# Merge gates' sigmoids at a fixed place in ScalarE's order, and the first merge gate's load ahead of part of the recurrence's output

## The chip, the cores and the metric

The kernel runs on one core of one Trainium2 chip. The metric is the device time of one execution in microseconds (us), as the median of several runs. A core has five engines that run their own instruction queues in order and meet through semaphores: TensorE (PE in the profile, with PEld for its weight loads), VectorE (DVE), ScalarE (ACT), GpSimd (POOL) and SyncE (SP), which in this kernel issues the DMAs. Matmul results land in eight banks of PSUM.

## The reference

One layer with two token mixers side by side, for 1024 tokens of width 1024, in float32:

```
h = rmsnorm(x, norm_g);  proj = h @ w_in      # split into q, k, v, decay code, gates, logits
o_gla = gla_chunked(...)                      # 4 heads, a recurrence with a decay per channel
o_gla = rmsnorm(o_gla, gla_norm_g) * silu(g_gate);   y_a = o_gla @ w_pa
o_sb = stick_breaking(...)                    # 8 heads, 128-query blocks, strictly causal
o_sb = o_sb * silu(s_gate);                          y_b = o_sb @ w_pb
gates = sigmoid(m_logits + b_gate)            # one gate per branch and channel
merged = gates[0] * y_a + gates[1] * y_b
return rmsnorm(x + merged @ w_o, final_g)
```

What the change touches is the term `gates[0] * y_a`: the sigmoid of the first branch's logits and its product with the projection of the recurrence's output.

## The kernel before

Everything lies transposed, channels on the 128 partitions and tokens along the free dimension, in two halves of 512 tokens. Each float32 operand is split into a rounded high part and a remainder, so that a product is three matmuls (high by high, high by low, low by high); `split` (L163) copies the high part on ACT and takes the difference on DVE.

The program is a chain of stages. An input stage norms and transposes x and projects it; the projections by blocks of two output panels follow (`pair_job`, L233), with the recurrence (`gl_...`, L861 to L1000) woven in. Results wait in DRAM: `d_ga` holds the logits of the first merge gate, `d_ogl` the recurrence's output, `d_q`, `d_k`, `d_v` the operands of the second mixer. Then comes the stage that matters here, the stick-breaking attention (L1025 to L1219), and behind it the two output projections.

The attention runs over 64 steps, 8 heads h by 8 query blocks i (L1205). A step does, in program order:

- every other step, the load of two later blocks' queries (`load_q`, L1021, tile `q`), and at i = 3 the load of the next head's keys and values (`load_head`, L1009 and L1012, tiles `k` and `v`);
- `scores` of the block two steps ahead: matmuls into a bank `z` (L1068 to L1070), in two halves of 320 to 512 columns where the block's prefix is over 512 long, a sigmoid of each half on ACT (L1071, tile `be`), and a running product on DVE (L1074). There are two `z` banks, and a half's bank is free when its sigmoid has run;
- `st.run`, which takes work from a hand-written list, below;
- `turn` of the block i: PE transposes (L1086) into `tr` and `pp` banks, split on ACT and DVE (L164 and L165, tiles `ath`, `atl`, `afh`, `afl`);
- at i = 2 the values of the previous head's second half and at i = 5 those of this head's first half (`values`, L1107 to L1114: matmuls into `av`, a product on DVE, a store to `d_osb`).

The list `line` (L1193 to L1198) is worked off one unit at a time, at i = 3 and i = 6 of heads 0, 1, 2, 4 and 6, and at i = 6 of the others. A unit is one projection of 24 matmuls (L203 to L205, bank `pp`). The entries that are not units (loads) run together with the unit ahead of them. First come four gates of the second mixer (`gate`); then `o_dma(1)`, the load of the second half of the recurrence's output as four transfers of 1 MB (L1189, tiles `oa21h`, `oa21l`, `oa22h`, `oa22l`); then the 16 units `pa(eb, n)`, the projection `y_a` of output panel eb and half n, each of which ends in `ma_half`. The first such unit runs at h = 1, i = 3, and the first that reads `oa21h` and its companions at h = 2, i = 6.

`ma_half` (L1157) first starts the load of the next unit's gate logits (`ga_load`, L1151, DMA at L1155 from `d_ga` into a tile `o`, one of three), then runs the sigmoid in that tile on ACT (L1161), the product with the projection on DVE (L1162), and the store to `d_ma` (L1163). The very first load is an entry of the list.

In this stage the order of the instructions on each engine is settled when the program is built, by a scheduler that works with estimated durations: it may put an instruction ahead of others that stand earlier in the program. The order on each engine is fixed from then on, and an instruction at the head of a queue that has to wait holds up all behind it. The stages behind L1460 are ordered by hand instead.

Of the kernel before, what the change touches and what calls it, by code (L numbers as in the profile page):

```python
# [11 lines left out]
AF = mybir.ActivationFunctionType  # L12
# [90 lines left out]
def hybrid_layer(ctx: ExitStack, tc: tile.TileContext, x, norm_g, w_in, w_up, b_dec,  # L103
# [5 lines left out]
    nc = tc.nc  # L109
# [43 lines left out]
    vcol = const.tile([P, 22], F32, tag="vcol", name="vcol")  # L153
# [13 lines left out]
    def half(n):  # L167
        return slice(n * HALF, (n + 1) * HALF)
# [146 lines left out]
    def quarter(pool, nm, tag):  # L315
        return tuple(pool.tile([P, 4, HALF], F32R, tag=tag + s, name=nm + s, bufs=1) for s in "hl")
# [239 lines left out]
    def silu(v, dst):  # L556
        o = stage().bitcast(F32)
        nc.scalar.activation(o[:, 0], v, AF.Sigmoid)
        nc.vector.tensor_mul(o[:, 1], v, o[:, 0])
        nc.sync.dma_start(dst, o[:, 1])  # L560
# [575 lines left out]
    def load(w, c0, key):  # L1136

        def go():
            raw = wk.pop(0) if wk else None
            ws[key] = load_w(w, c0, raw=raw)  # L1140
            if raw is not None:
                wk.append(raw)

        return (go, False)

    def unit(key, quads, n, fn):
        return (lambda: fn(proj_t(ws[key], quads, n)), True)
# [3 lines left out]
    def ga_load():  # L1151
        if len(ga) < len(halves):
            eb, n = halves[len(ga)]
            ga[eb, n] = stage().bitcast(F32)
            nc.sync.dma_start(ga[eb, n][:, 0], d_ga[eb][:, half(n)])  # L1155

    def ma_half(pt, eb, n):  # L1157

        ga_load()
        o = ga[eb, n]  # L1160
        nc.scalar.activation(o[:, 0], o[:, 0], AF.Sigmoid, bias=vcol[:, eb:eb + 1])  # L1161
        nc.vector.tensor_mul(o[:, 1], pt, o[:, 0])  # L1162
        nc.sync.dma_start(d_ma[eb][:, half(n)], o[:, 1])  # L1163

# [4 lines left out]
    def gate_load(h):  # L1169
        return load(w_in, C_SG + h * P, ("g", h))  # L1170

    def gate(h, n):
        return unit(("g", h), hq, n, lambda pt: silu(pt, d_sg[h][:, half(n)]))

    def pa_load(eb):
        return load(w_pa, eb * P, ("a", eb))

    def pa(eb, n):
        halves.append((eb, n))
        return unit(("a", eb), oq, n, lambda pt: ma_half(pt, eb, n))  # L1180

    def o_dma(n):

        def go():
            for e in range(2):
                nm = f"a{n + 1}{e + 1}"
                oq[n, e] = quarter(a21b if nm == "a21" else hp, "o" + nm, nm)
                for i in range(2):
                    nc.sync.dma_start(oq[n, e][i].bitcast(F32), d_ogl[e][:, i, :, half(n)])  # L1189

        return (go, False)

    line = [gate_load(6), gate_load(7), gate(6, 0), gate(7, 0), o_dma(0), gate(6, 1), pa_load(0), gate(7, 1), o_dma(1),  # L1193
            pa_load(1), (ga_load, False), pa_load(2), pa(0, 0), pa(1, 0), pa(2, 0)]
    for eb in range(5):
        line += ([pa(eb, 0)] if eb > 2 else []) + [pa(eb, 1), pa_load(eb + 3)]
    line += [pa(eb, n) for n in range(2) for eb in range(5, KB)]
# [433 lines left out]
```

## Time and profile before

| | us |
|---|---|
| median of 3 runs | 1179.27 |
| lowest and highest of them | 1178.54 and 1179.57 |
| the profiled execution | 1177.88 |
| its span in the profile | 1176.2 |

The profiled execution's span is the time from its first to its last recorded instruction; 1.7 us lie around it. The granted clock of TensorE over the span is 0.998 of full speed. All times of day below are microseconds from the span's start. In the views, L12 is line 12 of the kernel before; a row of a timeline gives the start, the duration, the engine, the line and operation, output and input tiles, and in brackets how long the engine sat idle before it and what it waited for.

### The profile page before, as it was taken

Reading aid. Unit: us, or ns where it says so; the run is one execution under the profiler, and the core shown is the slowest. Engines: PE = TensorE matmul, PEld = TensorE weight load, DVE = VectorE, ACT = ScalarE, POOL = GpSimd, SP = SyncE. Lnnn points to the kernel's source line nnn. Section 1 sums busy time; section 2 is a strip of 40 time slices with the busy share of each in tenths; the row PEclk is TensorE's granted clock in tenths of the full one; section 3 lists DMA queues with packets and bytes.
Section 4 is the critical chain, followed back from the end, with each engine's and each line's share of the span. In section 5 each row is a group of like instructions: output and inputs, shape, how many; then the busy total and the mean of one; then the engine's idle time right before and its main releaser. Section 6 shows DMA issues by size and latency. Waiting matters only on the chain.

```text
span 1176.2 us, 16650 instructions
## 1 busy us (share of the span) xinstructions
PE 1161.5 (99%) x5823; PEld 978.7 (83%) x5823; DVE 857.9 (73%) x1441; ACT 557.9 (47%) x1046; POOL 243.4 (21%) x217
## 2 busy tenths in 40 slices
PE   8999999999999999999999999999999999999997
PEld 7999888887888888888888878888888888888886
DVE  6797667888676886776665677456777876488986
ACT  6556663433544545545444443344444444364544
POOL 1022232334242242342242232000000000700001
PEclk9999999999999999999999999999999999999999
DMA  7325549997455664654543357789766556848652
GB/s 290 126 63 161 206 164 324 327 312 240 139 179 179 200 212 161 204 177 130 168 138 125 114 174 238 260 309 316 262 200 229 182 175 199 282 160 276 226 197 108
DMA packets 189456, 239.25 MB, mean 203 GB/s; under 512 B 12438, under 2 KB 128300, under 8 KB 187836
## 3 DMA queue, kind: packets, MB, share of 16 engines
q1 hardware_dynamic: 188796, 237.20, 60.8%
q8 instruction: 46, 0.75, 0.3%
q10 hardware_dynamic: 576, 0.98, 0.2%
q14 instruction: 38, 0.31, 0.1%
HBM read 150.06 MB, written 88.08 MB: 202 GB/s over the span
## 4 chain that ended last, share of the span: by engine, by line
PE 95%; DMA 2%; DVE 1%; ACT 1%; issue 1%; SPq 0%; POOLq 0%; POOL 0%; ACTq 0%
PE pp L269 17%; PE pp L270 17%; PE pp L271 17%; PE pp L204 3%; PE pp L203 3%; PE pp L205 3%; PE pp L222 2%; PE tr L1086 1%; PE z L1068 1%; PE av L1109 1%; PE av L1108 1%; PE av L1107 1%; DMA o<-d_ga 1%; PE z L1070 1%; PE z L1069 1%; PE xa L1362 1%
## 5 line engine op out<-in xcount | busy, mean ns | idle before, releaser
L269 PE MATMUL pp<-S,wh 128*128 128x512 f32 x372 | 147.0, 395 | 0.4 <-ACT f L275 0.4
L271 PE MATMUL pp<-S,wl 128*128 128x512 f32 x372 | 145.0, 390 | 0.0
L270 PE MATMUL pp<-S,wh 128*128 128x512 f32 x372 | 144.9, 389 | 0.0
L165 DVE TENSOR_TENSOR wl<-tt,wh 128x1024 fp32r<-128x1024 f32 x62 | 76.6, 1235 | 52.4 <-ACT wh L164 52.1
L308 DVE TENSOR_TENSOR f<-pp,f 128x512 f32<-128x512 f32 x93 | 64.0, 688 | 69.4 <-PE pp L271 63.0
L164 ACT ACTIVATE wh<-tt 128x1024 fp32r<-128x1024 f32 x62 | 65.6, 1059 | 75.0 <-PE pp L270 67.4
L243 POOL TENSOR_TENSOR tt<-raw 128x512 f32<-128x512 f32 x31 | 43.5, 1402 | 260.1 <-DVE wl L165 234.1
L275 ACT ACTIVATE f<-pp 128x512 f32<-128x512 f32 x93 | 55.0, 592 | 79.6 <-PE pp L271 74.1
L1074 DVE TENSOR_TENSOR_SCAN be<-be,m 128x128 f32<-128x128 f32 (+3 forms) x64 | 86.1, 1348 | 4.8 <-ACT be L1071 4.6
L164 ACT ACTIVATE wh<-raw 128x1024 fp32r<-128x1024 f32 (+1 forms) x47 | 48.4, 1030 | 84.6 <-PE pp L270 48.5
L269 PEld LDWEIGHTS pp<-S,wh 128*128 128x128 f32 x372 | 70.5, 189 | 14.7 <-ACT f L275 0.6
L271 PEld LDWEIGHTS pp<-S,wl 128*128 128x128 f32 x372 | 69.8, 188 | 14.8
L270 PEld LDWEIGHTS pp<-S,wh 128*128 128x128 f32 x372 | 69.9, 188 | 13.8
L165 DVE TENSOR_TENSOR wl<-raw,wh 128x1024 fp32r<-128x1024 f32 (+1 forms) x47 | 63.1, 1343 | 18.7 <-ACT wh L164 18.1
L230 POOL TENSOR_TENSOR r<-r,nhalf 128x1 f32<-128x1 f32 x40 | 25.2, 629 | 194.5 <-DVE r L229 194.5
L1268 POOL TENSOR_TENSOR N<-A,A 128x512 f32<-128x512 f32 x4 | 6.7, 1668 | 242.2 <-DMA A<-d_osb 242.2
L1071 ACT ACTIVATE be<-z 128x384 f32<-128x384 f32 (+4 forms) x96 | 46.9, 494 | 20.4 <-PE z L1070 18.3
L269 PE MATMUL pp<-ha11h,wh 128*128 128x512 f32 x124 | 49.2, 397 | 0.0
L269 PE MATMUL pp<-ha12h,wh 128*128 128x512 f32 x124 | 48.9, 395 | 0.0
L269 PE MATMUL pp<-ha22h,wh 128*128 128x512 f32 x124 | 48.7, 393 | 0.0
L164 ACT ACTIVATE dh<-raw 128x512 fp32r<-128x512 f32 x31 | 19.6, 631 | 61.4 <-PE pp L270 61.4
L269 PE MATMUL pp<-S,dh 128*128 128x512 f32 x124 | 48.6, 392 | 0.0
(546 smaller groups left out, 3425.5 us busy)
## 6 DMA issues: line engine op xcount, KB each, us to landing
raw<-in_w_in_dram SPq DMA_DIRECT2D x31, 1024.0 KB, 6.0
d_t<-t SPq DMA_DIRECT2D x16, 512.0 KB, 5.2
d_ogl<-o SPq DMA_DIRECT2D x64, 128.0 KB, 2.4
d_q<-o SPq DMA_DIRECT2D x16, 512.0 KB, 3.2
d_k<-o SPq DMA_DIRECT2D x16, 512.0 KB, 4.7
d_v<-o SPq DMA_DIRECT2D x32, 256.0 KB, 2.3
k<-d_k SPq DMA_DIRECT2D x8, 1024.0 KB, 7.1
v<-d_v SPq DMA_DIRECT2D x16, 512.0 KB, 4.9
```

The costliest lines, as they stand in the source:

```text
L164: nc.scalar.activation(hi, src, AF.Copy)
L165: eng.tensor_sub(lo, src, hi.bitcast(F32))
L203: nc.tensor.matmul(pt, whi[:, kb], h_, start=kb == 0, stop=False)
L204: nc.tensor.matmul(pt, whi[:, kb], l_, start=False, stop=False)
L243: nc.gpsimd.tensor_sub(t1, b[:, 0, 1], b[:, 0, 0])
L269: nc.tensor.matmul(pt, bh[:, j], ah[:, j], start=first and j == 0, stop=False, skip_group_check=True)
L270: nc.tensor.matmul(pt, bh[:, j], al[:, j], start=False, stop=False, skip_group_check=True)
L271: nc.tensor.matmul(pt, bl[:, j], ah[:, j], start=False, stop=j == 3, skip_group_check=True)
L275: nc.scalar.activation(t[nm], t[bank], AF.Copy)
L308: nc.vector.tensor_add(add, bank, add)
L1071: nc.scalar.activation(om[:, off + pc * w:off + (pc + 1) * w], zt[:, 0:w], AF.Sigmoid, scale=-inv_sqrt)
L1074: nc.vector.tensor_tensor_scan(rest, rest, m1[:, off:T][:, ::-1], 1.0, op0=ALU.mult, op1=ALU.max)
```

## The change

Two edits. The first wraps the sigmoid of `ma_half` so that the scheduler keeps it at its place in the program among ACT's instructions, where it stood free before. The second moves two entries of the list: the load of the first gate's logits and the two weight loads that stood behind `o_dma(1)` now stand ahead of it.

```diff
         ga_load()
         o = ga[eb, n]
-        nc.scalar.activation(o[:, 0], o[:, 0], AF.Sigmoid, bias=vcol[:, eb:eb + 1])
+        tc.keep_in_program_order(nc.scalar.activation(o[:, 0], o[:, 0], AF.Sigmoid, bias=vcol[:, eb:eb + 1]))
         nc.vector.tensor_mul(o[:, 1], pt, o[:, 0])
...
-    line = [gate_load(6), gate_load(7), gate(6, 0), gate(7, 0), o_dma(0), gate(6, 1), pa_load(0), gate(7, 1), o_dma(1),
-            pa_load(1), (ga_load, False), pa_load(2), pa(0, 0), pa(1, 0), pa(2, 0)]
+    line = [gate_load(6), gate_load(7), gate(6, 0), gate(7, 0), o_dma(0), gate(6, 1), pa_load(0), gate(7, 1),
+            (ga_load, False), pa_load(1), pa_load(2), o_dma(1), pa(0, 0), pa(1, 0), pa(2, 0)]
```

No instruction is added or removed, and POOL's order stays as it was.

On ACT, the first of the 16 sigmoids, at h = 1, i = 3 (`o<-o,vcol` is the gate's sigmoid, `ath` and `afh` the copies of `turn`, `be` the sigmoids of `scores`; - is the order before, + the order now):

```order
 L1071 ACTIVATE be<-z 128x384
-L164 ACTIVATE ath<-tr 128x4x128
-L1071 ACTIVATE be<-z 128x448
-L1161 ACTIVATE o<-o,vcol 128x512
-L1071 ACTIVATE be<-z 128x448
+L1161 ACTIVATE o<-o,vcol 128x512
+L164 ACTIVATE ath<-tr 128x4x128
+L1071 ACTIVATE be<-z 128x448 x2
```

The gate's sigmoid moved out from between the two halves of a block's scores to a place ahead of the copy of the transposes. Of the other 15, thirteen move to a later place and the last two stay: at i = 3 they now stand between the scores and the copies of `turn`, at i = 6 behind the first scores of the next head and ahead of the copies. The order before had pulled most of them ahead by one to three units, so that the place of the second unit held the third gate's sigmoid and that of the seventh unit, at h = 4, i = 6, the ninth gate's; now each unit holds its own.

On SP's queue, from step 6 of head 0 on (`d_sg` is a store, `v` and the `oa` tiles are loads):

```order
 L1189 DMA oa21h<-d_ogl_137 128x4x512
 L560 DMA d_sg_107<-o 128x512
+L1155 DMA o<-d_ga_139 128x512
 L1189 DMA oa21l<-d_ogl_137 128x4x512
 L1189 DMA oa22h<-d_ogl_138 128x4x512
 L1012 DMA v<-d_v_93 128x1024
 L1189 DMA oa22l<-d_ogl_138 128x4x512
-L1155 DMA o<-d_ga_139 128x512
```

The first gate's load passes three of the four transfers of the recurrence's output and the load of `v` between them; the fourth, `oa21h`, still stands ahead of it. One more pair on SP changes places: a load of keys (`k`, for head 3) now stands behind the store of `d_osb` that followed it.

On PE, one place changes, at i = 1 and i = 2 of head 2 (`av` are the values of the head before, `z` the scores of block 4; the piece ends one row before the old place of the three transposes):

```order
 L1086 MATMUL tr<-ident,be 128x128 x2
+L1068 MATMUL z<-k,q 128x320
+L1069 MATMUL z<-k,q 128x320
+L1070 MATMUL z<-k,q 128x320
 L1107 MATMUL av<-afh,v 128x512
 L1068 MATMUL z<-k,q 128x320
 L1069 MATMUL z<-k,q 128x320
 L1070 MATMUL z<-k,q 128x320
+L1086 MATMUL tr<-ident,be 128x128 x3
 L1108 MATMUL av<-afl,v 128x512
```

Both halves of the scores and the three transposes behind them now come earlier by one matmul of the values. On DVE, the product L1162 changes places with one neighbour at two places: at the first unit it now stands ahead of the remainder of `ath`, and at the twelfth, behind the attention, ahead of a remainder that the next stage reads.

## The prediction

> **What bounds the kernel.** The page first: the busy shares, then the chain of work that ended last.
>
> ```profile
> PE 1161.5 (99%) x5823; PEld 978.7 (83%) x5823; DVE 857.9 (73%) x1441; ACT 557.9 (47%) x1046; POOL 243.4 (21%) x217
> ...
> PE 95%; DMA 2%; DVE 1%; ACT 1%; issue 1%; SPq 0%; POOLq 0%; POOL 0%; ACTq 0%
> ```
>
> PE is the bound nearly everywhere: idle for 1176.2 - 1161.5 = 14.7 us in all. A change on ACT and SP can win only what PE stands still because of them, so the next view is the waits, of ACT over the whole span and then of PE between 770 and 1030 us, the attention and the projections behind it.
>
> ```profile
> ACT o L1161 <- DMA o<-d_ga: 45.1, 14, 6.1
> ...
> PE z L1068 <- ACT be L1071: 1.0, 1, 1.0
> PE tr L1086 <- DVE atl L165: 0.4, 2, 0.2
> ```
>
> The columns are total us, times, longest. ACT waits 45.1 us for the gate's loads, but PE loses only about 1.4 us in these 260. The timeline shows where: PE first, then ACT, then SP.
>
> ```profile
> 817.05 0.48 PE L1068 MATMUL z<-k,q 128*128 128x512 f32 x1
> 817.36 0.39 PE L1069 MATMUL z<-k,q 128*128 128x512 f32 x1
> 817.60 0.40 PE L1070 MATMUL z<-k,q 128*128 128x512 f32 x1
> 818.95 0.50 PE L1068 MATMUL z<-k,q 128*128 128x512 f32 x1 [0.96 <-ACT be L1071]
> 819.29 0.40 PE L1069 MATMUL z<-k,q 128*128 128x512 f32 x1
> ...
> 810.08 0.49 ACT L1071 ACTIVATE be<-z 128x384 f32<-128x384 f32 x1 [3.81 <-PE z L1070]
> 815.56 0.60 ACT L164 ACTIVATE ath<-tr 128x512 fp32r<-128x512 f32 x1 [4.99 <-PE tr L1086]
> 816.17 0.55 ACT L1071 ACTIVATE be<-z 128x448 f32<-128x448 f32 x1
> 817.74 0.72 ACT L1161 ACTIVATE o<-o,vcol 128x512 f32<-128x512 f32 x1 [1.02 <-DMA o<-d_ga]
> 818.37 0.52 ACT L1071 ACTIVATE be<-z 128x448 f32<-128x448 f32 x1
> ...
> 797.88 0.37 SPq L1189 DMA_DIRECT2D oa21h<-d_ogl  x1
> ...
> 801.67 0.43 SPq L1189 DMA_DIRECT2D oa21l<-d_ogl  x1
> ...
> 807.63 0.33 SPq L1012 DMA_DIRECT2D v<-d_v  x1
> 808.01 0.43 SPq L1189 DMA_DIRECT2D oa22l<-d_ogl  x1
> 808.49 0.50 SPq L1155 DMA_DIRECT2D o<-d_ga  x1
> ```
>
> Read backwards: PE's scores of block 7, second half, want the bank that the second half of block 6 holds. That half's sigmoid (818.37) stood behind the gate's sigmoid, which waited for its load. The load was issued at 808.49, behind a `v` load that SP held until 807.63. The chain says the same, with the landing:
>
> ```profile
> 808.49 9.17 DMA o<-d_ga
> ```
>
> So it landed at 808.49 + 9.17 = 817.66.
>
> **The change, part by part.** Part 1, the stop at 818. PE would have started the second half one matmul step behind 817.60, at 817.84 (the step from 817.36 to 817.60 was 0.24), and the next matmul at 818.08; it started at 819.29. The stop, with the restart, costs 819.29 - 818.08 = **1.21 us**. Is anything late in its place? The load now follows the store of `d_sg`, where `oa21l` was issued before, so it goes out at about 801.7. The rows near it:
>
> ```profile
> oa21h<-d_ogl SPq DMA_DIRECT2D x1, 1024.0 KB, 8.1
> oa22h<-d_ogl SPq DMA_DIRECT2D x1, 1024.0 KB, 9.9
> ...
> DMA to landing us min/median/max: 2.6/5.0/9.2
> ```
>
> (KB and us to landing; the last row is for the 16 gate loads.) From 801.7 the landing lies between 804.3 and 810.9; since `oa21h`, issued at 797.88, lands at 806.0 and 256 KB each of `d_sg` and the gate follow, I take 807.5. ACT comes to the sigmoid at its new place when it has done the scores of block 5 (810.08 + 0.49), about 810.6, and then has nothing until 815.56 (4.99 idle in the row above). The sigmoid's 0.72 us lie wholly there. The copy of `ath` starts at 815.56 as now and the first half's sigmoid at 816.17; the matmuls of the second half stand ahead of PE's row of 817.05, so its sigmoid starts by then at the latest and is done 0.52 later, by 817.6: before PE's 817.84. DVE's product L1162, now ahead of the remainder of `ath`, can run once PE's unit has ended, which is ahead of the transposes that ACT copies at 815.56; the remainder needs that copy, 816.16, so it is hardly delayed. Bounds for this part: 0 (something else holds PE) to 1.21; I take all, since no row shows another engine late there.
>
> Part 2, the other 15 sigmoids. The number of instructions and their durations stay; what changes is what stands behind a waiting one. The order before put them where the load has only just been issued; PE shows it at one place, head 4 to head 5. ACT there, and PE's transposes at the two ends of the same stretch, in head 1 to 2 (undisturbed) and in head 4 to 5:
>
> ```profile
> 908.39 0.72 ACT L1161 ACTIVATE o<-o,vcol 128x512 f32<-128x512 f32 x1 [5.16 <-DMA o<-d_ga]
> ...
> 828.19 0.49 PE L1086 MATMUL tr<-ident,be 128*128 128x128 f32 x3
> 833.35 0.55 PE L1086 MATMUL tr<-ident,be 128*128 128x128 f32 x3
> ...
> 908.23 0.49 PE L1086 MATMUL tr<-ident,be 128*128 128x128 f32 x3
> 913.59 0.55 PE L1086 MATMUL tr<-ident,be 128*128 128x128 f32 x3
> ```
>
> The stretch takes 833.35 - 828.19 = 5.16 us in one and 5.36 in the other, with one matmul less: **0.20 us** are due to the late sigmoid, and go, since the seventh unit's place now holds the seventh gate, loaded two units earlier. Bounds: 0 to 0.43 (that matmul's step of 0.23 counted too). Elsewhere the sigmoids land in ACT's idle time: at i = 3 in the 4.99 us above, at i = 6 in this:
>
> ```profile
> 822.96 0.28 ACT L1071 ACTIVATE be<-z 128x128 f32<-128x128 f32 x1 [1.04 <-PE z L1070]
> 826.07 0.73 ACT L1161 ACTIVATE o<-o,vcol 128x512 f32<-128x512 f32 x1 [2.84 <-DMA o<-d_ga]
> 828.71 0.49 ACT L164 ACTIVATE ath<-tr 128x384 fp32r<-128x384 f32 x1 [1.91 <-PE tr L1086]
> ```
>
> Between 823.2 and 828.7 PE does its 24 matmuls and ACT has nothing else. Without that cover a pinned sigmoid would cost up to 0.7 us in each of 11 steps. Behind the attention the twelfth to fourteenth sigmoids shift around the first copies of the next stage, and one DVE product goes ahead of one remainder of 0.69 us; PE is never idle there:
>
> ```profile
> 985.00:1030.00 45.00, 45.00 (x203) 37.23 (x202) 23.03 (x30) 17.29 (x27) 22.52 (x16) 1.00 0.78 262
> ```
>
> (us, then PE's busy time.) Cost 0.
>
> Part 3, the order of PE at head 2. The three transposes at 833.35 come behind one matmul of the values less, but what releases them is DVE:
>
> ```profile
> 829.23 0.56 DVE L165 TENSOR_TENSOR atl<-tr,ath 128x384 fp32r<-128x384 f32 x1 [0.16 <-ACT ath L164]
> ...
> 833.03 0.27 DVE L165 TENSOR_TENSOR atl<-tr,ath 128x128 fp32r<-128x128 f32 x1
> ```
>
> The last ends at 833.30, and between these two no row of DVE has idle time ahead of it, so it comes no earlier against the steps around it. PE will wait there for the matmul's length and do it afterwards: **-0.23 us** (bounds -0.23 and 0; I take the loss).
>
> Part 4, SP. The `oa` transfers behind the load wait one issue more, 0.5 us, and are read first a head later. The key load for head 3 now waits for the store ahead of it:
>
> ```profile
> 822.09 0.59 SPq L1009 DMA_DIRECT2D k<-d_k  x1
> 826.07 0.33 SPq L1114 DMA_DIRECT2D d_osb<-f  x1
> ...
> 850.73 0.28 PE L1068 MATMUL z<-k,q 128*128 128x256 f32 x1
> ```
>
> So it is issued some 4 us later, near 826.4, with what stands behind it 0.6 us later still. The same 1 MB took 8.1 and 9.9 us above; it lands by 836.3, and is read at 850.73. Cost 0, with 14 us to spare.
>
> Sum: 1.21 + 0.20 - 0.23 = 1.18 us. The profiled execution took 1177.88 us (span 1176.2 and 1.7 around it), so 1176.7; the runs' median, 1179.27, is 1.39 above it, so **1178.1**.
>
> One rule of the Trainium skill, in sentences the sum does without. Perfetto Trace Analysis, section Identifying the Most-Contended Engine, calls matmul busy time a bad measure of what is left to gain and goes by the share of weight loads. By it the window with the stop, the first row below, has 8.00 - 6.16 = 1.84 us free, and the sum would be 1.81 instead of 1.18, a time inside rival (c). The trace agrees only in part: the 24 us behind it, where PE is idle for 0.04 in all, have loads for 86%, so that of the 1.84 us only 0.86 x 8.00 - 6.16 = 0.72 are the stop's.
>
> ```profile
> 818.00:826.00 8.00, 7.05 (x39) 6.16 (x40) 7.50 (x12) 4.20 (x10) 0.00 (x0) 1.00 0.75 213
> 826.00:850.00 24.00, 23.96 (x134) 20.67 (x133) 15.74 (x25) 12.23 (x26) 0.00 (x0) 1.00 0.75 263
> ```
>
> **The rivals.** (a) *The stop stays under another name*, or the load's new place does not help: PE's second half waits for `be` all the same, or the matmul behind it for a bank that DVE frees. For it: DVE is busy for 7.50 of the 8 us. Against: its work there (scan, remainders) starts earlier too once the scores' sigmoid does. Then only parts 2 and 3 are left, -0.03: 1179.3.
>
> (b) *The pinned sigmoid comes late for its new place*, and holds the copy and both halves behind it. The load took 9.17 us before, longer than any of the other 15. It decides from about 815: ACT has to be free at 815.56, and the sigmoid holds it for 0.63 us. If it landed at 817.66 as now, the copy would start at 818.4, the first half's sigmoid at 819.0, done at 819.5; PE, which wants that bank at 817.05, would stand for 2.5 us instead of 1.1. That is 1.4 + 0.03 lost: 1180.7, and 1 us more for each us of delay. Against: it would have to take 13 us from its issue, where the slowest row shows 9.9.
>
> (c) *More is freed than I count.* PE's waits between 770 and 1030 are the one on ACT and two on DVE behind ACT, 1.4 us together, and a wait costs more than its bracket: 1.21 for 0.96 above, so 0.25 for the restart. If all three went, and part 3 cost nothing, that would be 1.4 + 3 x 0.25 = 2.15: 1177.1. For it: ACT loses its sigmoid from each of these clusters. Against: at head 2 DVE has no gap to close.
>
> **How the numbers follow.** Forecast 0.62, (a) 0.17, (c) 0.14, (b) 0.07. The runs lie from 0.7 below to 0.3 above their median. The low end is (c) less about half of that, 1176.7; the upper end is (a) with its scatter and some of (b), 1180.2; it leaves out most of (b) and little else. What a measurement can tell from no change is about 0.2%, 2.4 us: faster means below 1176.9, which only (c) with low runs reaches, 0.10; slower above 1181.6, the far end of (b), 0.05; within, 0.85.
>
> **What would show it.** Right: in the profile after, the first gate's load is issued near 801.7 and its sigmoid starts near 810.6 with little idle time ahead of it for the load; PE's row of block 7 has no bracket and the row `PE z L1068 <- ACT be` is gone; the chain has no load of `d_ga` at 808 or 901; ACT's 45.1 us of waiting for `d_ga` fall below 18: only the last three can still wait, at most 6.1 each as now. The stretch at head 5 takes 5.16 us, and at head 2 PE waits on `atl` ahead of the three transposes. Wrong: a bracket of about a microsecond on another row between 816 and 823, a sigmoid that starts after 815, or a wait for `k` at head 3.

## The result, and the profile after

The changed kernel takes **1176.9 us** (median of 20 runs, 1176.35 to 1178.54; a few executions that were disturbed, by hundreds of us and more, are left out here and below), the kernel before, run beside it, 1179.57 (21 runs, 1177.95 to 1182.26). The ratio is 0.9977, with a 95% interval of 0.9970 to 0.9984: 2.67 us are gone, a little over the 2.4 that the prediction counted as telling from no change; the interval puts the gain between 1.9 and 3.5 us. The forecast was 1178.1, a gain of 1.2. The profiled execution, by contrast, did what the forecast said to a few hundredths: 1176.68 against 1177.88, span 1175.0 against 1176.2. So two questions stand: where the 1.2 us of the trace came from, and why the medians moved by more than twice as much.

The page of the changed kernel, busy shares and the chain by engine:

```profile
PE 1162.1 (99%) x5823; PEld 979.5 (83%) x5823; DVE 857.2 (73%) x1441; ACT 558.3 (48%) x1046; POOL 244.3 (21%) x217
...
PE 96%; DVE 2%; DMA 1%; ACT 1%; issue 1%; SPq 0%; POOLq 0%; POOL 0%; ACTq 0%; DVEq 0%
```

PE's busy time is 0.6 us more than before; what is gone is idle time, 1175.0 - 1162.1 = 12.9 us instead of 14.7. The waits, of ACT for the gates' loads over the span and of PE between 770 and 1030 us (total us, times, longest):

```profile
ACT o L1161 <- DMA o<-d_ga: 14.2, 3, 6.1
...
PE tr L1086 <- DVE atl L165: 0.2, 1, 0.2
```

PE's wait for `be` has no row any more, and of ACT's 45.1 us only three waits are left, behind the attention. The timeline at the place of the old stop, ACT, then PE, then SP:

```profile
810.52 0.71 ACT L1161 ACTIVATE o<-o,vcol 128x512 f32<-128x512 f32 x1
815.60 0.60 ACT L164 ACTIVATE ath<-tr 128x512 fp32r<-128x512 f32 x1 [4.37 <-PE tr L1086]
816.22 1.16 ACT L1071 ACTIVATE be<-z 128x448 f32<-128x448 f32 x2
...
817.64 0.40 PE L1070 MATMUL z<-k,q 128*128 128x512 f32 x1
817.88 0.40 PE L1068 MATMUL z<-k,q 128*128 128x512 f32 x1
818.11 0.39 PE L1069 MATMUL z<-k,q 128*128 128x512 f32 x1
...
801.71 0.42 SPq L1155 DMA_DIRECT2D o<-d_ga  x1
```

The load goes out at 801.71, the sigmoid starts at 810.52 with no idle time ahead of it, and the two halves of a block's sigmoids now run as one piece (x2). PE goes from the first half of block 7 to the second without a stop: 818.11 - 817.64 = 0.47 where it was 819.29 - 817.60 = 1.69, 1.22 us less. The two stretches between heads, PE, and one row of DVE in the first:

```profile
827.01 0.49 PE L1086 MATMUL tr<-ident,be 128*128 128x128 f32 x3
832.17 0.55 PE L1086 MATMUL tr<-ident,be 128*128 128x128 f32 x3
...
837.03 0.34 PE L1068 MATMUL z<-k,q 128*128 128x384 f32 x1
...
907.24 0.49 PE L1086 MATMUL tr<-ident,be 128*128 128x128 f32 x3
912.41 0.55 PE L1086 MATMUL tr<-ident,be 128*128 128x128 f32 x3
...
831.85 0.26 DVE L165 TENSOR_TENSOR atl<-tr,ath 128x128 fp32r<-128x128 f32 x1
```

At head 2 the stretch between the transposes still takes 5.16, now with one matmul of the values less in it, and up to the scores behind the values it takes 837.03 - 827.01 = 10.02, where before it was 9.79: 0.23 lost. What holds the second transposes is DVE, as the prediction said, though too shortly for a bracket: its row ends at 831.85 + 0.26 = 832.11, they start at 832.17. At head 4 to 5 it takes 5.17 instead of 5.36: 0.19 won. Together 1.22 - 0.23 + 0.19 = 1.18, the forecast's sum.

### The profile page after: what moved, and what is told of

The parts are those of the page before. It is cut to its first block, busy times and chain, and to the rows that moved or that the text cites. A ratio compares the mean times of both kernels' runs of the same rounds, so it can differ in the third digit from the quotient of the medians.

```text
span 1175.0 us, 16650 instructions
## 1 busy us (share of the span) xinstructions
PE 1162.1 (99%) x5823; PEld 979.5 (83%) x5823; DVE 857.2 (73%) x1441; ACT 558.3 (48%) x1046; POOL 244.3 (21%) x217
## 4 chain that ended last, share of the span: by engine, by line
PE 96%; DVE 2%; DMA 1%; ACT 1%; issue 1%; SPq 0%; POOLq 0%; POOL 0%; ACTq 0%; DVEq 0%
PE pp L269 17%; PE pp L270 17%; PE pp L271 17%; PE pp L204 3%; PE pp L205 3%; PE pp L203 3%; PE pp L222 2%; PE av L1108 2%; PE av L1109 2%; PE tr L1086 1%; PE av L1107 1%; PE z L1068 1%; PE z L1070 1%; PE z L1069 1%; PE xa L1363 1%; PE xa L1362 1%
## 5 line engine op out<-in xcount | busy, mean ns | idle before, releaser
L164 ACT ACTIVATE wh<-raw 128x1024 fp32r<-128x1024 f32 (+1 forms) x47 | 48.4, 1030 | 84.0 <-PE pp L270 48.5
```

Source lines behind the costliest of these rows:

```text
L164: nc.scalar.activation(hi, src, AF.Copy)
```

## Experiments

Two theories for the rest. **L**: the places where a sigmoid stands behind its own load cost what the landing makes of it in each execution, and the profiled one was lucky. **P**: it is gained elsewhere, in every execution. Each run gives one more profile. All runs of one group shared the runs of the kernel before. F, K and C in the later expectations are theories about one place each. The ratios in the tables are worked out from all runs of both kernels and are not those of the two medians.

**The kernel before again, and each edit alone.** `e1` has no edit. `e2` has only the first edit, `e3` only the second:

```diff
-        nc.scalar.activation(o[:, 0], o[:, 0], AF.Sigmoid, bias=vcol[:, eb:eb + 1])
+        tc.keep_in_program_order(nc.scalar.activation(o[:, 0], o[:, 0], AF.Sigmoid, bias=vcol[:, eb:eb + 1]))
```

```diff
-gate(7, 1), o_dma(1), pa_load(1), (ga_load, False), pa_load(2), pa(0, 0), pa(1, 0), pa(2, 0)]
+gate(7, 1), (ga_load, False), pa_load(1), pa_load(2), o_dma(1), pa(0, 0), pa(1, 0), pa(2, 0)]
```

> The kernel before once more, with its profile. The question for all four runs: the medians moved by 2.67 us, the profiled executions by 1.20. Theory L (landing): before, two gate loads end in waits of PE (issued at 808.49 and about 901), so each us that they land later than in the first profile is about a us of time, and most executions have them later than the profiled one (1177.88, near the lowest of its runs, 1177.95 to 1182.26). Theory P (place): the 1.4 us that the traces do not explain are gained elsewhere in the program, in every execution. L expects of this profile: span minus 1176.2 equals the change of the wait at block 7's scores (0.96 us then) plus that of the stretch from head 4 to 5 (5.36 then), within 0.2 us; times 1178 to 1182, wider than those after. P expects that the span moves, if it does, by something outside these two places.

> The first edit alone: the sigmoids pinned, the list as before, so the first load is still issued near 808.5 behind the transfers of the recurrence's output. By the steps of the prediction: the stop at block 7's scores stays (1.2 us), the stretch from head 4 to 5 takes 5.16, the loss of 0.23 at head 2 stays; a profile within 0.3 us of that of before, 1177.9, if the load lands alike. L: what is left exposed is one load, so the times stay spread over 2 us or more and the median is 0 to 1 us below before. P: the unexplained 1.4 us come with whichever edit makes them; if with this one, the times lie 1.4 us below before with the stop still there.

> The second edit alone: the first load ahead of three of the four transfers, the sigmoids free. By the steps of the prediction: the stop at block 7's scores is gone (1.2 us won), the stretch from head 4 to 5 stays at 5.36, head 2 keeps its order and loses nothing: profile about 1176.7. The first sigmoid stands ahead of the copy of block 3 here, near 806, and may hold ACT for a microsecond or two until its load is there. L: the load at 808 was the larger part of what varies; median 1.2 to 2.3 us below before, spread between those of before and after. P: if the 1.4 us come with this edit, the full 2.6 us below before, with a spread like that of before.

> The changed kernel once more, beside the others on the same chip. L: profile at 1176.7 plus or minus 0.3, since no load ends in a wait of PE; times within 1 us of each other; median 2 to 3 us below before. P: median 2.7 us below before as well, but the spread no narrower than that of before.

| run | median us (lowest to highest) | against before, ratio (95%) |
|---|---|---|
| before, beside these | 1179.48 (1177.37 to 1180.63) | |
| e2, sigmoids pinned | 1177.71 (1176.78 to 1180.04) | 0.9988 (0.9979 to 0.9996) |
| e3, list only | 1178.93 (1178.07 to 1181.91) | 1.0004 (0.9995 to 1.0012) |
| e4, both again | 1177.01 (1176.25 to 1178.73) | 0.9983 (0.9975 to 0.9992) |

The medians fit neither theory throughout. `e4` repeats the gain, 2.47 us, but its times lie 2.5 us apart and not within 1 as L expected, hardly less than the 3.3 of before, as P expected. `e2` gains 1.77 where L expected 0 to 1, and `e3` 0.55, with an interval on both sides of nothing, where L expected 1.2 to 2.3. So the profiles have to decide. The kernel before, run again as `e1`, `e8`, `e9` and `e10`, comes out at 1.0000 to 1.0006, each interval on both sides of 1.

The profile of `e1` took 1179.15 (span 1177.3), 1.1 us more than the first one. ACT at head 4, the chain's row of the load, and PE's transposes:

```profile
909.53 0.72 ACT L1161 ACTIVATE o<-o,vcol 128x512 f32<-128x512 f32 x1 [6.21 <-DMA o<-d_ga]
...
901.34 8.12 DMA o<-d_ga
...
908.32 0.49 PE L1086 MATMUL tr<-ident,be 128*128 128x128 f32 x3
914.72 0.55 PE L1086 MATMUL tr<-ident,be 128*128 128x128 f32 x3
```

The ninth gate's load took 8.12 us to land instead of 7.07, 1.05 more, and the stretch 914.72 - 908.32 = 6.40 instead of 5.36, 1.04 more. That is the whole difference between the two profiles but 0.1, as L expects. The 0.20 that the prediction took for this place was low.

`e2` did better than its own steps said: the first load was issued at 808.65, as late as before, yet the stop was small, because in this execution it landed in time:

```profile
817.03 0.72 ACT L1161 ACTIVATE o<-o,vcol 128x512 f32<-128x512 f32 x1
...
808.65 8.29 DMA o<-d_ga
```

Landing at 816.94, 0.7 us sooner than before, the load let the sigmoid start right behind the first half's, and PE's step took 818.57 - 817.78 = 0.79 instead of 1.69. `e3` did worse, and here the miss is the prediction's own. The old stop is gone (step 0.46), but there is a new one at head 2, ACT, then PE, then SP:

```profile
831.52 0.72 ACT L1161 ACTIVATE o<-o,vcol 128x512 f32<-128x512 f32 x1 [2.19 <-DVE afl L165]
...
832.67 0.41 PE L1068 MATMUL z<-k,q 128*128 128x320 f32 x1 [1.99 <-ACT be L1071]
...
824.24 0.43 SPq L1009 DMA_DIRECT2D k<-d_k  x1
824.77 0.40 SPq L1155 DMA_DIRECT2D o<-d_ga  x1
```

This is the fourth gate's sigmoid, which, where it is free, stands ahead of a block's scores. The row names DVE, whose remainder `afl` started at 829.87 and took 0.68; it had been done for a microsecond, so what ended the wait was the load: the trace's semaphore records have its last completion at 831.45. With the list changed, the 1 MB of keys leaves SP half a microsecond ahead of that load, where in the kernel before it left 4.4 ahead, at 822.09 (a row of the prediction) against:

```profile
826.50 0.37 SPq L1155 DMA_DIRECT2D o<-d_ga  x1
```

The second edit alone trades a stop of 1.2 us for one of 2.

**One sigmoid at a time.** Three runs move one sigmoid of ACT's order (and in `e7` PE's order at head 2, which goes back to that of before). `e5` and `e7` are the changed kernel with the ninth or the fourth sigmoid free, `e6` the kernel before with the ninth pinned; `e8` is the kernel before.

```diff
-        tc.keep_in_program_order(nc.scalar.activation(o[:, 0], o[:, 0], AF.Sigmoid, bias=vcol[:, eb:eb + 1]))
+        (tc.keep_in_program_order if len(ga) != 10 else id)(nc.scalar.activation(o[:, 0], o[:, 0], AF.Sigmoid, bias=vcol[:, eb:eb + 1]))
```

(`len(ga) != 5` in `e7`, `len(ga) == 10` in `e6`.)

> The changed kernel with one sigmoid left free, the ninth, which goes back to its place in head 4, behind its own load; one instruction of ScalarE has moved and nothing else. Theory L (the cost of a sigmoid behind its load is what the landing makes of it): the stretch from head 4 to 5 grows from 5.16 by 0.2 to 1.3 us, since the load landed 7.07 us after its issue in one profile of before and 8.12 in the other, and its stretch was 5.36 and 6.4; median 0.5 to 1.3 us above the changed kernel. Theory F (the first profile was typical, the prediction's 0.20 holds): 0.2 us above it.

> The kernel before with that one sigmoid pinned: one instruction of ScalarE moved, no other. L: the stretch from head 4 to 5 takes 5.16 instead of 5.36 to 6.4; the stop at block 7's scores stays; median 0.5 to 1.3 us below before. F: 0.2 below.

> The changed kernel with the fourth sigmoid left free: it goes back ahead of the scores of block 3 in head 2, behind its own load, and TensorE's order in head 2 is that of before. Theory K (the load of keys, 1 MB, which the second edit put right ahead of the fourth gate's load, makes that load land 6 to 7 us after its issue): a stop of about 2 us at head 2, as in the run of the second edit alone, median 1.5 to 2.2 us above the changed kernel. The prediction's own steps (the later load of keys costs nothing; the order of head 2 costs 0.23): no stop there, and 0.23 us below the changed kernel.

> The kernel before, a third profile. L: what its span has over the first one's 1176.2 is the delay at the three places where a sigmoid stands behind its load (block 7's scores in head 1, the fourth in head 2, the stretch from head 4 to 5) and the start, up to 100 us; outside of these and of the recurrence's loads TensorE runs the same to 0.1 us.

| run | median us (lowest to highest) | against before, ratio (95%) |
|---|---|---|
| before, beside these | 1178.94 (1177.11 to 1180.61) | |
| e5, after, ninth free | 1177.54 (1176.36 to 1180.00) | 0.9991 (0.9982 to 1.0000) |
| e6, before, ninth pinned | 1178.14 (1176.24 to 1180.17) | 0.9992 (0.9983 to 1.0001) |
| e7, after, fourth free | 1178.57 (1177.58 to 1180.70) | 0.9998 (0.9989 to 1.0006) |

Pinning the ninth in the kernel before brings 0.80 us by the medians, inside L's range, but the interval, 2.0 us faster to 0.1 slower, also holds F's 0.2. In its profile the stretch takes 5.16, as expected. The stop at block 7's scores, which was expected to stay, is not there (0.55 in the table below): the first gate's load landed sooner in this execution, 8.13 us from its issue to the sigmoid's start at 816.07 instead of 9.25, and the sigmoid ran without idle time ahead of it. Freeing the fourth leaves 0.37 of the gain, where both edits together had 2.47 in the group before (the changed kernel did not run in this one): 2.1 are given back, as K expects. Its profile has the stop where K put it. At 1.15 us it is smaller than the 2 expected, since the load landed sooner than in `e3`:

```profile
831.03 0.72 ACT L1161 ACTIVATE o<-o,vcol 128x512 f32<-128x512 f32 x1 [1.35 <-DVE afl L165]
...
832.18 0.42 PE L1068 MATMUL z<-k,q 128*128 128x320 f32 x1 [1.15 <-ACT be L1071]
```

So PE's order at head 2 by itself was not worth 0.23 there: the late sigmoid ate it. `e5` is 1.40 below before, so against those 2.47 it gives back 1.1, inside L's range. But its profile, 1180.0, was the slowest of its runs, and its loss at the place, 7.66 - 5.17 = 2.5 us, was twice the most that L expected (the expectation of `e11` puts it at 2.9; the rows give 2.5). Two windows behind the ninth sigmoid (us, busy time of PE, PEld, DVE, ACT and POOL, then PE's granted clock, the share of DMA and GB/s):

```profile
909.00:913.00 4.00, 2.46 (x16) 1.63 (x13) 2.65 (x5) 3.78 (x9) 0.00 (x0) 1.00 0.49 147
913.00:917.00 4.00, 4.00 (x17) 3.63 (x16) 4.00 (x6) 1.83 (x5) 0.00 (x0) 0.57 0.58 185
```

PE stood for 1.54 us in the first window, and in the next its clock was 0.57. Its rows show two waits and then the slow matmuls, 0.27 apart for 320 columns where the changed kernel's are 0.14 to 0.15 apart (911.72, 911.86, 912.01):

```profile
910.96 0.33 PE L1086 MATMUL tr<-ident,be 128*128 128x128 f32 x1 [0.88 <-DVE atl L165]
...
912.77 0.48 PE L1086 MATMUL tr<-ident,be 128*128 128x128 f32 x2 [0.67 <-DVE atl L165]
...
913.31 0.47 PE L1069 MATMUL z<-k,q 128*128 128x320 f32 x1
913.58 0.47 PE L1070 MATMUL z<-k,q 128*128 128x320 f32 x1
```

**More profiles.** Two of the kernel before and one more of `e5`'s kernel:

> The kernel before, a fourth profile. In the first three the stretch from head 4 to 5 lost 0.2, 1.2 and 1.0 us against the changed kernel's, in step with the start of the ninth sigmoid. L: here too it loses about 1 us, 0.8 to 1.3, and the loss follows the sigmoid's start one for one; the stop at block 7's scores 1.1 to 1.2; the first profile's 0.2 was the low end. F: 0.2 to 0.5 here.

> The kernel before, a fifth profile, with the same expectation as the fourth.

> The changed kernel with the ninth sigmoid free, a second profile. In the first its stretch from head 4 to 5 lost 2.9 us, of which the sigmoid's start explains 1.8; behind it TensorE's granted clock was 0.57 for 4 us. Theory C (the clock adds the rest): without a drop of the clock the loss is what the start of the sigmoid gives, 0 to 1.8 us by the landing; with a drop, about 1 us more. Rival: the order itself costs more there than in the kernel before, and the loss is 1 us above the line of the profiles of before with the clock at 1.00.

In `e11` (1178.34 against 1179.47, ratio 0.9989, 0.9978 to 1.0001) the sigmoid started 0.73 us behind the first row of the transposes, the clock stayed at 1.00, and the stretch took 5.92, on the line of the kernel before (below): theory C, not its rival.

```profile
908.14 0.72 ACT L1161 ACTIVATE o<-o,vcol 128x512 f32<-128x512 f32 x1 [5.11 <-issue]
...
909.00:913.00 4.00, 3.33 (x22) 2.66 (x20) 3.73 (x6) 3.79 (x10) 0.00 (x0) 1.00 0.60 197
913.00:917.00 4.00, 3.91 (x20) 3.09 (x19) 3.56 (x6) 0.97 (x3) 0.00 (x0) 1.00 0.41 133
```

All profiles side by side. Each place is measured between two rows of PE, and the sigmoid's start against the first of them, so that shifts from earlier in the program drop out. A: from the last matmul of block 7's first half to the second of its second half (817.60 to 819.29 in the first profile). B: from the three transposes of head 1 to the first scores behind the values (828.19 to 837.98). C: from the three transposes of head 4 to those of head 5 (908.23 to 913.59). "Late" is the start of the first, fourth and ninth gate's sigmoid less that first row; "-" where the sigmoid doesn't stand there. All us.

| profile | late 1 | A | late 4 | B | late 9 | C | A + B + C |
|---|---|---|---|---|---|---|---|
| before, first | 0.14 | 1.69 | 2.72 | 9.79 | 0.16 | 5.36 | 16.84 |
| before, e1 | 0.14 | 1.67 | 2.95 | 9.91 | 1.21 | 6.40 | 17.98 |
| before, e8 | 0.00 | 1.55 | 2.73 | 9.76 | 0.98 | 6.18 | 17.49 |
| before, e9 | 0.51 | 2.06 | 2.92 | 9.88 | 0.79 | 5.99 | 17.93 |
| before, e10 | -0.13 | 1.41 | 3.72 | 10.66 | 0.78 | 5.97 | 18.04 |
| e6, ninth pinned | -0.99 | 0.55 | 3.40 | 10.36 | - | 5.16 | 16.07 |
| e2, all pinned | -0.75 | 0.79 | - | 10.03 | - | 5.16 | 15.98 |
| e3, list only | - | 0.46 | 5.04 | 11.96 | 1.10 | 6.29 | 18.71 |
| e7, fourth free | - | 0.46 | 4.19 | 11.13 | - | 5.16 | 16.75 |
| e11, ninth free | - | 0.47 | - | 10.02 | 0.73 | 5.92 | 16.41 |
| e5, ninth free | - | 0.46 | - | 9.98 | 1.81 | 7.66 | 18.10 |
| after, first | - | 0.47 | - | 10.02 | - | 5.17 | 15.66 |
| after, e4 | - | 0.46 | - | 10.03 | - | 5.16 | 15.65 |

Read a column pair downwards. A is late 1 plus 1.55, to 0.02, in all seven profiles that have it. C is late 9 plus 5.19, to 0.01, in all but `e5`, the one with the dropped clock, which lies 0.66 above it. B is late 4 plus 6.95, to 0.03, from 2.9 on, and some 9.8 at the least. **Once a sigmoid that waits for its load is late enough to hold PE, it costs PE one microsecond for each microsecond that the load lands later, at all three places**, and only A was seen in full by the first profile.

With both edits none of the three is there: the two profiles after agree to 0.01 in the sum. Of what the spans of before have over the first one's 1176.2 (`e1` 1.1, `e8` 0.9, `e9` 2.6, `e10` 3.1) the three places give 1.14, 0.65, 1.09 and 1.20; 1.5 in each of `e9` and `e10` come from the first 20 us (last section), and the rest, up to 0.4, from the recurrence's loads near 289 us (PE waits there for ACT, which waits for a load from `d_gv`: 0.39 in the first profile, 0.73 in `e8`, 0.86 in `e10`). Held row against row, PE's 5823 rows stand in the same order in all five, and they part by more than 0.15 us nowhere else. Up to 805 us PE's order is the same in every kernel here, and the eight profiles of the kernels with an edit lie there between 0.55 us ahead of the first profile of before and 0.39 behind it, `after` 0.04 behind. That is theory L; P, a gain in every execution somewhere else, has nothing left but the 0.5 to 0.7 us below.

## Why the prediction was right or wrong

- **What bounds it**: right. PE was idle for ACT, and ACT for the gates' loads.
- **Part 1, 1.21 us**: right, 1.22 in the first pair of profiles and 0.94 to 1.59 in the other four of before. The load landed at 807.48 by the semaphore records, the 807.5 assumed, and the sigmoid started at 810.52 in idle time, as said. The 1.1 to 1.2 expected of `e9` and `e10` for this stop was too narrow: they have 1.59 and 0.94.
- **Part 2, 0.20 us: here the size failed.** The mechanism and the place were right, but the step "The stretch takes 833.35 - 828.19 = 5.16 us in one and 5.36 in the other" took one execution's landing for a property of the kernel, and "Bounds: 0 to 0.43" bounded the count of matmuls, not the landing. The five profiles of before give 5.36, 6.40, 6.18, 5.99 and 5.97, 0.8 us above 5.17 in the mean and 1.2 at the most.
- **Part 3, -0.23**: right for the pair of profiles (10.02 against 9.79), and by the wait for `atl` that it named. It missed that the same place held a third exposed sigmoid, the fourth, which costs up to 0.9 more in the kernel before (10.66 in `e10`) and which the pin also removes. In the mean of the five, B is 10.00, so there the change neither wins nor loses.
- **Part 4, 0**: right for the changed kernel, whose `k` load at 824.76 delays nobody. But "Cost 0, with 14 us to spare" looked only at the reader of `k`. The gate's load is queued behind it, and where the fourth sigmoid is free (`e3`, `e7`) it came 5.9 to 6.8 us after its issue, against 4.4 to 5.4 in the profiles that have `k` further ahead. That the bytes of `k` are the reason was not tried apart.
- **The sum and the last step.** 1.18 was the difference of the profiled executions. The step "the runs' median, 1179.27, is 1.39 above it" carried the scatter of the kernel before over to the changed one. That scatter was in part the very thing the change removes: the sum A + B + C of the first profile is 16.84, the lowest of five, and their mean is 17.66, against 15.66 after: 2.0 us. The medians say 2.67 beside the first runs and 2.47 in the second group, so 0.5 to 0.7 us stay unexplained. The rest of the program does vary by more than that: the drop of the clock at the start (below) is in two of the five profiles of before and in none of the eight others, which would make 2/5 x 1.5 = 0.6. But both come from one group of runs, the program is the same there in all kernels, and so few profiles cannot tell this from chance. The measured 1176.9 lies inside the stated range, but near its low end, 1176.7, which had been set for rival (c): with the mechanism right and the gain sized from one lucky execution, that the number fell inside is in part luck.
- **The rivals.** (a) and (b) fell: no row of PE waits for `be`, and the sigmoid starts 5 us ahead of the time from which it would hurt. (c) gave 1177.1, near what was measured, but not by its mechanism: it had both waits on DVE go and the 0.23 at head 2 come back. The wait on `atl` at 912 us is gone, but the one at 779 us, 0.2 us, is there as before, and in this pair of profiles the 0.23 is lost.
- **The rule on weight loads**: in the window from 818 to 826, PE now is busy for all 8.00 us with weight loads for 6.92. So by the share of weight loads, which the Trainium skill's Perfetto Trace Analysis, section Identifying the Most-Contended Engine, goes by, 1.08 us would still be free in a window in which PE never stands. The 0.72 that the prediction put down to the stop came out as 6.92 - 6.16 = 0.76.

```profile
818.00:826.00 8.00, 8.00 (x45) 6.92 (x44) 6.68 (x11) 3.00 (x7) 0.00 (x0) 1.00 0.68 237
```

The two edits, then: the pin does most of it, 1.77 us by the medians of `e2`. Taking the ninth sigmoid from behind its load accounts for 0.8 of that against the mean of before; the rest its profile has at A, by a first load that landed early, which the pin did not bring. The list alone does nothing that can be measured, as it leaves C exposed and makes B worse. With the pin it removes what is left of A. No run has a lower median than the changed kernel. Its remaining loss of 0.23 at head 2 would need the fourth sigmoid pinned and PE's order of before at once; that was not tried.

## What to carry to other kernels

An instruction that waits for a load at the head of an in-order queue has no fixed cost: measure its lateness against the engine it holds up, and price it over several profiles, since one profile may be the lucky one. When a change hides such a load, expect the medians to move by another amount than one pair of profiles shows: here by more, since the profiled execution of the kernel before had the least lateness of five. That the scatter shrinks as well is not shown: the times spread over 2.2 us instead of 4.3 beside the first runs, but over 2.5 against 3.3 in `e4`. And when an order is changed, look at each load that is queued behind a moved transfer, not only at the moved transfer's own reader.

## What the runs showed of the hardware that was not expected

The same load of 256 KB, issued 7.0 us ahead of head 4's transposes each time, landed after 7.07, 8.12, 7.89, 7.69 and 7.69 us in five executions of one kernel (the ninth gate), and the first gate's, issued 9.1 ahead of A's first row, after 9.17, 9.16, 9.03, 9.54 and 8.91.

PE's granted clock fell in one run behind two short stops, and in others it did not fall behind longer ones. In `e5` its mean was 0.57 over 4 us, behind two waits of 0.88 and 0.67 us between transposes; in `e3` a single wait of 1.99 us left it at 1.00:

```profile
830.00:834.00 4.00, 2.00 (x11) 1.56 (x12) 1.90 (x4) 2.35 (x6) 0.00 (x0) 1.00 0.90 327
834.00:838.00 4.00, 4.00 (x23) 3.48 (x22) 3.08 (x4) 1.57 (x3) 0.00 (x0) 1.00 0.86 267
```

The Trainium skill's TensorE: Matmul & The Clock Gate, section Why this matters for your kernels, asks that idle gaps of PE stay below some 3 us; `e5` shows a drop with none above 0.88 near it, and the measurement decides. What sets it off is not shown. A drop was also seen at the start of the program in two of the profiles of before, `e9`'s first 20 us against the first profile's:

```profile
0.00:20.00 20.00, 16.04 (x88) 14.63 (x89) 10.03 (x16) 10.76 (x17) 3.36 (x10) 0.91 0.92 338
...
0.00:20.00 20.00, 15.31 (x101) 13.87 (x102) 10.61 (x19) 11.77 (x20) 3.91 (x11) 1.00 0.92 339
```

With the clock at 0.91 in the mean, PE ran 88 matmuls in that time instead of 101, and all of the program behind it came 1.5 us later. It lies 800 us ahead of the changed places. Taken in finer windows the three drops are alike: the clock is 0.50 from 913.05 to 916.40 in `e5`, from 13.60 to 16.90 in `e9` and from 13.50 to 16.80 in `e10`. PE's longest wait just ahead of it, 1.28 us at 12.13 in `e9`, is there in the first profile too (1.30 at 12.14), without a drop.
